# One decoder layer on one core: a new load order in the opening, sums moved to VectorE, a weight block loaded into its sum's tile, and a narrower widest level

## The chip, the cores and the metric

The kernel runs on one core of a Trainium2 chip. Five engines work side by side, each through its own queue in order: TensorE (PE in the profile, its weight loads PEld), VectorE (DVE), ScalarE (ACT), GpSimd (POOL) and SyncE (SP), which here only starts transfers. The metric is the device time of one execution in microseconds (us). The last section before the prediction gives the time before.

## The reference

One layer over 16 learned meta tokens and 1024 real ones, width 1024, in float32:

```
h = h + 1/2 * SwiGLU_1(RMSNorm(h))           # 1024 -> 2 x 2816 -> 1024
u = RMSNorm(h) @ W_in
o = concat[ HGRN2(u_hgrn), StickBreaking(u_sb) ]
h = h + o @ W_out
h = h + 1/2 * SwiGLU_2(RMSNorm(h))
```

HGRN2 has 4 heads of 128. Within a block of 128 positions it needs, for each query t and key s ≤ t, a score of q and k weighted by the product of the forget gates from s+1 to t:

```
decay = exp(bcum[t] - bcum[s])   where s <= t
attn  = einsum('td,sd,tsd->ts', q, k, decay)
o     = attn @ v + (q * exp(bcum)) @ S ;  S carried from block to block
```

Stick-breaking attention has 8 heads of 64. The output is the layer's h without the meta tokens.

## The kernel before, in words

Float32 products are made of three products of split operands: each operand x becomes a high part `xh` (an ACT cast) and a rest `xl` (a DVE subtraction), and PE adds wh·xh + wl·xh + wh·xl (`times`, L309; L599).

The 1040 positions are cut into a plain third of 272 and two wide ones of 384 (`THIRDS`). In both FFNs the two wide halves are multiplied by a Strassen-Winograd scheme: seven products of half-size blocks in place of eight. It needs sums of weight blocks (S1 = A21 + A22, S2 = S1 − A11, A11 − A21, A12 − S2) and sums of the operand's blocks (T1 to T4). In `fast_in` (the FFN's first product) a *quad* is seven such products, each 12 matmuls of 384 columns; a *pair* is a gate quad and an up quad. POOL makes the weight sums of `fast_in` (`made`, L281). When a pair is complete, `combined` (L435) makes four sums of its activations, T1 to T4, each followed by a store that POOL issues (`put`).

**The opening** (L1384 to L1437). The plain rows are loaded, normalised and turned (`first_plain`). The plain third is then multiplied for the first five pairs, block by block (`plain_quad`): 40 steps of 12 matmuls of 272 columns, each with a weight block of 256 KB from a ring of eight. In between, the rows of the two wide blocks are loaded (`rows_of`, three tiles of 128 rows each, on SP), normalised (`norm_rows`: a sum of squares for each tile, then for all three together one square root on ACT and a reciprocal, then one scaling on DVE for each tile) and turned by PE (`first_block`: 24 transposes for a block, in groups of 6, two plain steps between groups). Each block has its own root. Then the five *opened* pairs run over the wide blocks, and after them the other pairs with plain and wide parts together.

**What sets the order.** PE's instructions stand in the order in which they are written out. For the other engines and for SP's transfers a planner orders the instructions by its own costs, by priority (`high_priority`) and by when a tile comes free; `issue_after(x)` puts what is written inside it behind x on x's engine. So a load on SP's queue can stand in front of one that is needed sooner, and a load that waits for a tile holds up what is behind it.

**The FFN's second product** (`fast_out`, L491). Seven steps (A12, A11, S1, S2, S4, S3, A22), each eleven blocks long, each block with a weight tile and an activation tile. `raw` (L506) loads a weight block into a ring of five tiles (six in the second FFN). `left` (L525) gives a step its operand; A11 blocks are loaded straight into the wide tile `ak`, S1 is made into the wide tile `sk` from two ring tiles (L537), and S2 is made from both (L540).

**HGRN2** (`hgrn_attend`, L825) makes the scores of a block level by level: level n covers, in each stretch of 2n positions, the keys of the first half and the queries of the second. `scores` (L851) multiplies all 128 keys of a block by all 128 queries for four blocks into one score tile (pool `pz`, two tiles), and `level` (L870) copies out what belongs to the level, for n ≥ 16 by ACT (L877). After each level q and k are multiplied by the gates' products on DVE. Three heads run side by side, the fourth after the first, woven by `weave` with the first half of the mixing product (`mix_out`), whose operand `oT` is loaded from memory (L1649, three tiles).

**Before the second FFN** the rows are normalised by `row_norm` (L227), which multiplies by the row `g2r` of gains; that row is loaded by `gain_row` (L222) where it is first needed (L1709).

Of the kernel before, what the change touches and what calls it, by code (L numbers as in the profile page):

```python
# [20 lines left out]
P = 128  # L21
# [18 lines left out]
class Block:  # L40
# [212 lines left out]
    def fast_in(self, ops, n, w_in, actD, openers, ev0, open_ev, feed=None, plain=None,  # L253
# [19 lines left out]
        def block(i, h, col):  # L273
            t = self.wraw.tile([P, 4, P], F32, tag="raw", name="raw", bufs=self.in_bufs)
            self.last_w = nc.sync.dma_start(
                t, w_in[512 * h : 512 * h + 512, col + P * i : col + P * i + P]
                .rearrange("(k p) f -> p k f", p=P)
            )
            return t
# [122 lines left out]
        def pair(f, opened=None, also=(None, None)):  # L402
            sg = {}
# [31 lines left out]
            def combined():  # L435

                sub = nc.gpsimd.tensor_sub
# [53 lines left out]
    def fast_out(self, out_of, n, w_out, actD, load_h, ready, between=lambda a, q: None,  # L491
# [33 lines left out]
        def left(step, q):  # L525
# [10 lines left out]
            if step == "S1":  # L536
                nc.vector.tensor_add(s, raw(1, 0, q), raw(1, 1, q))  # L537
                return s
# [77 lines left out]
    def load_rows(self, eng, row, r0, m, cols=slice(0, D)):  # L616

        x, meta = self.a["x"][0], self.a["meta_tokens"]
        if r0 == 0:
            eng.dma_start(row[:META], meta[:, cols])  # L620
            eng.dma_start(row[META:m], x[: m - META, cols])
        else:
            eng.dma_start(row[:m], x[r0 - META : r0 - META + m, cols])

    def rows_of(self, ci, pool, eng):
# [3 lines left out]
        for r0 in range(c0, c0 + n, P):  # L629
            m = min(P, c0 + n - r0)  # L630
            row = pool.tile([P, D], F32, tag="row", name="row", bufs=self.row_bufs)
            self.load_rows(eng, row, r0, m)
# [23 lines left out]
    def norm_rows(self, ci, rows, junk, whole=False):  # L656

        nc = self.nc
        sums = self.ss[:, 3 * ci : 3 * ci + 3]

        def square(i, row, m):
            s = sums[:m, i, 0:1]
            if i == (1 if whole else 2):
# [13 lines left out]
        for i, (row, at, m) in enumerate(rows):  # L677
# [4 lines left out]
        if whole:  # L682
            root(P, slice(0, 3))
            for i, (row, at, m) in enumerate(rows):
# [140 lines left out]
    def hgrn_attend(self, h, pool, src, oH):  # L825
# [43 lines left out]

        def level(i, n):  # L870
            nb = P // (2 * n)
# [480 lines left out]
    def run(self):  # L1352
# [20 lines left out]
        with ExitStack() as c0:  # L1373
            with ExitStack() as c1:
                with tc.manual_schedule(engines={nc.tensor.engine}), ExitStack() as c2:
# [28 lines left out]

                    steps = self.fast_in(
# [7 lines left out]
                    with tc.high_priority():  # L1413
                        with tc.issue_after(self.last_w.ins):
                            rows.append(self.rows_of(2, rp, nc.sync))
                        with tc.issue_after(self.last_x.ins):
                            self.norm_rows(2, rows[1], junk, True)
                    drain(islice(steps, 4))
                    with tc.high_priority():
                        with tc.issue_after(self.last_w.ins):  # L1420
                            rows.append(self.rows_of(1, rp, nc.sync))
                        with tc.issue_after(self.root.ins):
                            self.norm_rows(1, rows[2], junk, True)
# [429 lines left out]
```

## Time and profile before

| | |
|---|---|
| runs | 2064.38, 2059.65, 2064.20 us; median 2064.2 |
| the profiled execution's own time | 2062.77 us |
| its span, first to last instruction | 2061.0 us |
| granted TensorE clock, mean | 1.000 |
| busy: PE, DVE, ACT, POOL | 2004.8, 1376.6, 901.2, 638.6 us |
| chain that ended last: PE, DVE, DMA | 83%, 7%, 3% |

The stages of this execution follow from the timeline: the plain steps of the opening from 14 to 86 us, the opened pairs from 86 to about 241, the other pairs to about 489; the first FFN's second product from 489 to about 710, its S1 step from about 600; projections and stick-breaking to about 1215; HGRN2 woven with the first half of the mixing product to about 1365; the second half with the norm to about 1420; the second FFN from there, its second product from 1847.

How to read a row: a line of the timeline gives start, length, engine, line of the kernel, operation, output and inputs, and in brackets the idle time just ahead of it with the engine and instruction that ended it. A row of grouped instructions gives how many there are, then busy time, mean length in ns and the idle time ahead of them. A row of waits gives who waited for whom: us in total, times, longest. PE's matmuls are pipelined, so the recorded length of one is longer than the distance to the next; distances between starts tell its pace.

### The profile page before, as it was taken

The page shows a single profiled execution, that of the slowest core. Times are in us where ns is not written, and L with a number is a line of the kernel's source. Part 1 is how long each engine was busy: PE and PEld are TensorE (multiplying, and loading weights), DVE is VectorE, ACT ScalarE, POOL GpSimd, SP SyncE. Part 2 cuts the span into 40 slices and gives each one's busy share as a digit, 9 for nine tenths or more (in the row PEclk, how much of TensorE's full clock was granted, in tenths as well). Part 3 has the DMA queues.
Part 4 walks back from the last instruction along what each step waited for, and adds up shares of the span by engine and source line. Part 5 has one row for each costly group of instructions (what it writes and reads, how often), then busy time and mean ns, then how long its engine had stood idle before and what let it go on. Part 6 is the DMA issues. An engine that isn't in the chain of part 4 may idle for free.

```text
span 2061.0 us, 31571 instructions
## 1 busy us (share of the span) xinstructions
PE 2004.8 (97%) x11249; PEld 1782.3 (86%) x11249; DVE 1376.6 (67%) x2069; ACT 901.2 (44%) x1855; POOL 638.6 (31%) x696
## 2 busy tenths in 40 slices
PE   7999999999999999999999999999999999999999
PEld 7999999999987899988887878888888888878887
DVE  6867745556688842257878757648677677666774
ACT  7633332334554534456666623336333333234443
POOL 2366644542000002243443300210564454441000
PEclk9999999999999999999999999999999999999999
DMA  8643322227875645435454262684343333349573
GB/s 237 192 145 113 112 79 94 99 76 232 285 219 171 226 135 169 147 123 130 116 144 114 64 223 88 195 272 137 112 131 105 95 110 102 97 150 346 185 229 113
DMA packets 289647, 314.96 MB, mean 153 GB/s; under 512 B 24080, under 2 KB 218000, under 8 KB 289488
## 3 DMA queue, kind: packets, MB, share of 16 engines
q1 hardware_dynamic: 272304, 260.83, 41.1%
q0 software_dynamic: 16144, 52.10, 6.6%
q8 instruction: 89, 1.46, 0.3%
q14 instruction: 70, 0.57, 0.1%
q10 hardware_dynamic: 1040, 0.00, 0.0%
HBM read 228.62 MB, written 84.23 MB: 152 GB/s over the span
## 4 chain that ended last, share of the span: by engine, by line
PE 83%; DVE 7%; DMA 3%; ACT 3%; issue 2%; POOL 0%; SPq 0%; DVEq 0%; POOLq 0%; ACTq 0%
PE o L599 16%; PE qb L313 15%; PE qa L313 10%; PE qc L313 10%; PE proj L162 5%; PE proj L160 5%; PE proj L161 5%; PE qd L313 4%; PE o L561 3%; PE wo L1267 3%; PE flip L1086 2%; DVE wl L270 1%; PE lvl L855 1%; DVE keep L1232 1%; PE oacc L1156 1%
## 5 line engine op out<-in xcount | busy, mean ns | idle before, releaser
L313 PE MATMUL qb<-T,wh 128*128 128x384 f32 (+1 forms) x1056 | 317.8, 362 | 0.0
L270 DVE TENSOR_TENSOR wl<-s,wh 128x512 fp32r<-128x512 f32 x176 | 198.8, 1130 | 95.2 <-ACT wh L268 91.1
L313 PEld LDWEIGHTS qb<-T,wh 128*128 128x128 f32 x1056 | 195.8, 188 | 21.5
L313 PE MATMUL qa<-B,wh 128*128 128x384 f32 (+1 forms) x704 | 213.9, 367 | 0.3 <-ACT sg L415 0.3
L599 PE MATMUL o<-wl,th 128*128 128x512 f32 x539 | 209.9, 391 | 3.7 <-DVE wl L520 3.7
L599 PE MATMUL o<-wh,tl 128*128 128x512 f32 x539 | 209.6, 390 | 0.7 <-DVE tl L520 0.7
L599 PE MATMUL o<-wh,th 128*128 128x512 f32 x539 | 209.9, 391 | 0.0
L268 ACT CAST wh<-s 128x512 fp32r<-128x512 f32 x176 | 109.4, 621 | 223.2 <-PE qb L313 164.1
L160 PE MATMUL proj<-xh,wh 128*128 128x384 f32 (+2 forms) x576 | 205.0, 356 | 0.2 <-ACT xh L250 0.2
L270 DVE TENSOR_TENSOR wl<-raw,wh 128x512 fp32r<-128x512 f32 x184 | 170.1, 926 | 52.2 <-ACT wh L268 48.7
L161 PE MATMUL proj<-xh,wl 128*128 128x384 f32 (+2 forms) x576 | 199.1, 346 | 0.0
L162 PE MATMUL proj<-xl,wh 128*128 128x384 f32 (+2 forms) x576 | 198.9, 345 | 0.1
L268 ACT CAST wh<-raw 128x512 fp32r<-128x512 f32 x184 | 113.6, 620 | 184.1 <-PE qc L313 100.4
L313 PE MATMUL qb<-T,wl 128*128 128x384 f32 (+1 forms) x528 | 192.0, 364 | 0.9 <-DVE wl L270 0.9
L518 ACT CAST th<-act 128x512 fp32r<-128x512 f32 (+2 forms) x176 | 96.6, 550 | 178.1 <-PE o L599 120.0
L520 DVE TENSOR_TENSOR tl<-act,th 128x512 fp32r<-128x512 f32 (+2 forms) x176 | 105.5, 602 | 64.9 <-ACT th L518 63.7
L313 PE MATMUL qd<-X,wh 128*128 128x272 f32 x704 | 144.4, 292 | 2.0 <-DVE sp L397 1.6
L283 POOL TENSOR_TENSOR s<-raw 128x512 f32<-128x512 f32 x88 | 122.6, 1393 | 74.8 <-DVE wl L270 60.1
L313 PEld LDWEIGHTS qa<-B,wh 128*128 128x128 f32 x704 | 130.5, 188 | 16.5 <-ACT sg L415 0.7
L1232 DVE TENSOR_TENSOR_SCAN keep<-keep 128x144 f32<-128x144 f32 (+6 forms) x112 | 127.1, 1138 | 8.3 <-ACT keep L1228 6.0
L1237 POOL TENSOR_TENSOR sig<-sig,keep 128x144 f32<-128x144 f32 (+3 forms) x64 | 88.2, 1378 | 141.7 <-DVE keep L1232 75.6
L313 PE MATMUL qa<-B,wl 128*128 128x384 f32 (+1 forms) x352 | 128.8, 366 | 0.8 <-DVE wl L270 0.8
(343 smaller groups left out, 4761.1 us busy)
## 6 DMA issues: line engine op xcount, KB each, us to landing
raw<-in_ffn_w_in_dram SPq DMA_DIRECT2D x228, 256.0 KB, 3.0
raw<-in_ffn_w_out_dram SPq DMA_DIRECT2D x176, 256.0 KB, 4.3
raw<-in_w_in_dram SPq DMA_DIRECT2D x28, 512.0 KB, 4.5
ks<-kD SPq DMA_DIRECT2D x32, 260.0 KB, 5.6
oT<-oD SPq DMA_DIRECT2D x32, 256.0 KB, 4.7
ak<-in_ffn_w_out_dram SPq DMA_DIRECT2D x22, 256.0 KB, 5.3
v<-vD SPq DMA_DIRECT2D x8, 576.0 KB, 4.8
vD<-vhl SPq DMA_DIRECT2D x8, 512.0 KB, 3.9
```

The source lines that it names most:

```text
L160: nc.tensor.matmul(ps, wh[:, s], xs, start=k == 0, stop=False)
L161: nc.tensor.matmul(ps, wl[:, s], xs, start=False, stop=False)
L162: nc.tensor.matmul(ps, wh[:, s], xl[:, k, c0 : c0 + n], start=False, stop=k == nk - 1)
L268: nc.scalar.copy(hi, src)
L270: nc.vector.tensor_sub(lo, src, hi.bitcast(F32))
L283: op(t, x, y)
L313: nc.tensor.matmul(ps, a[:, k, :], b[:, k0 + k, :], start=start and k == 0 and i == 0, stop=k == 3 and i == 2, skip_group_check=True,)
L518: nc.scalar.copy(hi, src)
L520: nc.vector.tensor_sub(lo, src, hi.bitcast(F32))
L599: nc.tensor.matmul(banks[bank][m], z[:, m * P : (m + 1) * P], y, start=start and q == 0 and e == 0, stop=q == nq - 1 and e == 2, skip_grou ...
L1232: nc.vector.tensor_tensor_scan(out=kv, data0=kv, data1=kv, initial=1.0 if last else keep[:, end : end + 1], op0=ALU.mult, op1=ALU.bypass,)
L1237: nc.gpsimd.tensor_mul(sig, sig, keep[:, 1 : nk + 1])
```

## The change

- *Opening.* Both wide blocks' rows are loaded before either is normalised: the second block's (`ci` 2) after the first eight steps' weights, the other's after the next four steps'. Weight loads written after a block's rows stand behind these on SP's queue (`rows_ahead`, the last row's load). `norm_rows` takes all six row tiles: two of the six sums of squares are on DVE, four on ACT, and there is one root over six columns.
- *Opened pairs.* Their four sums are made by DVE in place of POOL; the stores stay on POOL's queue. The later pairs and the second FFN keep POOL.
- *S1.* The block A21 is loaded straight into its place in `sk`, and A22 from the ring is added to it there; in both FFNs.
- *Widest level* (n = 64). 64 keys by 64 queries for each of the eight blocks, into one score tile of 64 partitions, and one copy in place of two.
- *Before the second FFN.* The row `g2r` is loaded ahead of HGRN2, into the pool that holds h; `oT` has four tiles instead of three.

```diff
         def block(i, h, col):
             t = self.wraw.tile([P, 4, P], F32, tag="raw", name="raw", bufs=self.in_bufs)
-            self.last_w = nc.sync.dma_start(
-                t, w_in[...].rearrange("(k p) f -> p k f", p=P)
-            )
+            with ExitStack() as behind:
+                if self.rows_ahead:
+                    behind.enter_context(self.tc.issue_after(self.rows_ahead.ins))
+                self.last_w = nc.sync.dma_start(
+                    t, w_in[...].rearrange("(k p) f -> p k f", p=P)
+                )
             return t
...
         def pair(f, opened=None, also=(None, None)):
+            opening = plain and also == (None, None)
...
-                sub = nc.gpsimd.tensor_sub
+                sub = (nc.vector if opening else nc.gpsimd).tensor_sub
...
             if step == "S1":
-                nc.vector.tensor_add(s, raw(1, 0, q), raw(1, 1, q))
+                nc.sync.dma_start(s, block(1, 0, q))
+                nc.vector.tensor_add(s, s, raw(1, 1, q))
                 return s
...
-    def norm_rows(self, ci, rows, junk, whole=False):
+    def norm_rows(self, at, rows, junk, whole=False):
-        sums = self.ss[:, 3 * ci : 3 * ci + 3]
+        sums = self.ss[:, at : at + len(rows)]
-            if i == (1 if whole else 2):
+            if i % 3 == (1 if whole else 2):
-            root(P, slice(0, 3))
+            root(P, slice(0, len(rows)))
...
+        def widest():
+            ps = self.pz.tile([P // 2, 8, P // 2], F32, tag="z", name="lvl")
+            for c in range(8):
+                s = META + c * P
+                nc.tensor.matmul(
+                    ps[:, c, :], KB[:, s : s + P // 2], QA[:, c * P + P // 2 : (c + 1) * P],
+                    start=True, stop=True,
+                )
+            nc.scalar.copy(at8[: P // 2, :, P // 2 :], ps)
+
         def level(i, n):
+            if 2 * n == P:
+                return widest()
...
-                    with tc.high_priority():
-                        with tc.issue_after(self.last_w.ins):
-                            rows.append(self.rows_of(2, rp, nc.sync))
-                        with tc.issue_after(self.last_x.ins):
-                            self.norm_rows(2, rows[1], junk, True)
-                    drain(islice(steps, 4))
-                    with tc.high_priority():
-                        with tc.issue_after(self.last_w.ins):
-                            rows.append(self.rows_of(1, rp, nc.sync))
-                        with tc.issue_after(self.root.ins):
-                            self.norm_rows(1, rows[2], junk, True)
+                    for ci in (2, 1):
+                        with tc.high_priority(), tc.issue_after(self.last_w.ins):
+                            rows.append(self.rows_of(ci, rp, nc.sync))
+                        self.rows_ahead = self.last_row
+                        if ci == 2:
+                            drain(islice(steps, 4))
+                    with tc.high_priority(), tc.issue_after(self.last_x.ins):
+                        self.norm_rows(3, rows[1] + rows[2], junk, True)
...
                     hb = self.pool("hb", ctx=c1)
+                    gain = self.gain_row(a["ffn2_norm"][0:1], hb, "g2r")
...
-                        t = self.pool_o.tile([P, 2, 4, P], F32R, tag="oT", name="oT", bufs=3)
+                        t = self.pool_o.tile([P, 2, 4, P], F32R, tag="oT", name="oT", bufs=4)
...
-                    gain = self.gain_row(a["ffn2_norm"][0:1], pn, "g2r")
```

More of the change, by code (lines that the diff above doesn't have):

```diff
@@ L274, in block @@
             t = self.wraw.tile([P, 4, P], F32, tag="raw", name="raw", bufs=self.in_bufs)
-            self.last_w = nc.sync.dma_start(
-                t, w_in[512 * h : 512 * h + 512, col + P * i : col + P * i + P]
-                .rearrange("(k p) f -> p k f", p=P)
-            )
+            with ExitStack() as behind:
+                if self.rows_ahead:
+                    behind.enter_context(self.tc.issue_after(self.rows_ahead.ins))
+                self.last_w = nc.sync.dma_start(
+                    t, w_in[512 * h : 512 * h + 512, col + P * i : col + P * i + P]
+                    .rearrange("(k p) f -> p k f", p=P)
+                )
             return t
@@ L620, in load_rows @@
             eng.dma_start(row[:META], meta[:, cols])
-            eng.dma_start(row[META:m], x[: m - META, cols])
-        else:
-            eng.dma_start(row[:m], x[r0 - META : r0 - META + m, cols])
+            return eng.dma_start(row[META:m], x[: m - META, cols])
+        return eng.dma_start(row[:m], x[r0 - META : r0 - META + m, cols])
     def rows_of(self, ci, pool, eng):
@@ L631, in rows_of @@
             row = pool.tile([P, D], F32, tag="row", name="row", bufs=self.row_bufs)
-            self.load_rows(eng, row, r0, m)
+            self.last_row = self.load_rows(eng, row, r0, m)
             got.append((row, r0 - c0, m))
@@ L675, in root @@
             nc.vector.reciprocal(r, r)
-        for i, (row, at, m) in enumerate(rows):
+        for i, (row, _, m) in enumerate(rows):
             square(i, row, m)
@@ L682, in norm_rows @@
         if whole:
-            root(P, slice(0, 3))
-            for i, (row, at, m) in enumerate(rows):
+            root(P, slice(0, len(rows)))
+            for i, (row, _, m) in enumerate(rows):
                 nc.vector.tensor_scalar_mul(row, row, sums[:, i, 1:2])
@@ L1403, in between @@
                         next(turning[0], None)
+                    self.rows_ahead = None
                     steps = self.fast_in(
@@ L1431, in run @@
                             next(steps)
+                    self.rows_ahead = None
                     drain(steps)
```

## The prediction

> **What bounds the kernel now.** I read the page first, then the tensor engine's waits by stage, then the timeline of the engine that each wait names.
>
> ```profile
> span 2061.0 us, 31571 instructions
> PE 2004.8 (97%) x11249; PEld 1782.3 (86%) x11249; DVE 1376.6 (67%) x2069; ACT 901.2 (44%) x1855; POOL 638.6 (31%) x696
> ```
>
> The tensor engine (PE) is busy 97% of the span, so there are two ways to gain: close one of its holes, of which there are 2061.0 − 2004.8 = 56 us in all, or give it less to do. The change touches five places with holes. The profiled execution took 2062.77 us, 1.8 around its span, and the median of the runs is 2064.2; the sum is made against 2062.77, and a change is judged against 2064.2. About 0.3%, 6.2 us, is what a measurement of this kernel can tell from none.
>
> **A. The opening's load order and the single root.** Its two larger holes are 0.94 + 1.63 = 2.6 us:
>
> ```profile
> 31.66 0.39 PE L313 MATMUL qd<-X,wl 128*128 128x272 f32 x1 [0.94 <-DVE wl L270]
> 49.28 0.36 PE L313 MATMUL qd<-X,wh 128*128 128x272 f32 x1 [1.63 <-DVE sp L397]
> 20.00:40.00 20.00, 19.06 (x152) 18.84 (x152) 13.41 (x33) 14.63 (x27) 5.49 (x11) 1.00 0.89 276
> 40.00:60.00 20.00, 17.94 (x139) 16.91 (x138) 17.59 (x38) 19.27 (x39) 1.63 (x3) 1.00 0.59 150
> 25.11 1.06 ACT L668 ACTIVATE junk<-row 128x1024 bf16<-128x1024 f32 x1
> 26.79 1.28 ACT L672 ACT_TABLE_LOAD   x1
> 28.09 0.30 ACT L672 ACTIVATE ss_x<-ss_x,eps 128x3 f32<-128x3 f32 x1
> 33.48 0.46 SPq L623 DMA_DIRECT2D row<-in_x_dram  x1
> row<-in_x_dram SPq DMA_DIRECT2D x7, 512.0 KB, 5.3
> 34.66 0.82 PE L648 MATMUL xps<-ident,row 128*128 128x128 f32 x6
> ```
>
> (The window rows give start:end, length, then busy time and count of PE, PEld, DVE, ACT and POOL, the granted clock, the DMA share and GB/s.) The larger hole falls in 40 to 60 us, where ACT is busy 19.27 of 20.00 us and DVE 17.59. The second block's squares, root and scaling are done there; the change moves them forward, and two roots become one. That removes a root (0.30) and two table loads of 1.28 (to the root's table and back), 2.9 us of ACT's work where it is full. [...]
>
> The price is on the first block: its scaling now waits until the sixth row tile has landed. On SP's queue the new order is eight weight blocks, three row tiles, four weight blocks, three row tiles, the rest. Up to the sixth tile that is 1.1 MB (the plain rows) + 12 × 0.26 + 6 × 0.52 = 7.4 MB, at 276 GB/s 26.8 us of transfer: it lands at 28, or somewhat later. A square (1.06) and the table load (1.28) then put the root at about 31 instead of 28.09. In the trace 6.6 us pass from the root's start to the transposes at 34.66; with as much again they would come at 38 at the latest, where the tensor engine arrives at 33.7 if the first hole is gone. So the new hole is 0 to 4.3 us; I take 1.4, since the transposes take the tiles one after another, and 2.0 of the old holes recovered: **0.6**. The ends are 0.94 − 4.3 = −3.4 and 2.6. Weight blocks queued behind rows are covered by the eight that are loaded ahead.
>
> **B. The opened pairs' sums on VectorE.**
>
> ```profile
> PE qc L313 <- DVE wl L270: 1.9, 1, 1.9
> PE qb L313 <- DVE wl L270: 0.9, 3, 0.4
> PE qc L313 <- DVE sg L417: 0.5, 3, 0.2
> 123.20 1.31 POOL L283 TENSOR_TENSOR s<-raw,s 128x512 f32<-128x512 f32 x1
> 124.46 1.01 POOL L444 TENSOR_TENSOR t<-sg,t 128x384 f32<-128x384 f32 x1
> 125.44 1.28 POOL L283 TENSOR_TENSOR s<-raw 128x512 f32<-128x512 f32 x1
> 123.79 3.48 DVE L270 TENSOR_TENSOR wl<-raw,wh 128x512 fp32r<-128x512 f32 x1 [1.07 <-ACT wh L268]
> 132.80 0.69 DVE L270 TENSOR_TENSOR wl<-raw,wh 128x512 fp32r<-128x512 f32 x1
> 126.72 0.34 PE L313 MATMUL qb<-T,wh 128*128 128x384 f32 x1
> 127.33 0.44 PE L313 MATMUL qb<-T,wl 128*128 128x384 f32 x1 [0.27 <-DVE wl L270]
> L427 DVE TENSOR_TENSOR sg<-u,sg 128x384 f32<-128x384 f32 x14 | 7.7, 551 | 0.0
> L440 POOL DMA_DIRECT2D act10T<-t x3: 547/552/552, 119.6 to 126.7; - x3
> DMA to landing us min/median/max: 2.1/2.1/2.2
> ```
>
> From 85 to 241 us the tensor engine waits seven times in the gate half of a pair, while POOL catches up with the previous pair's four sums. At 123.79 a subtraction that takes 0.69 us alone takes 3.48: it ends as the third of POOL's three adjoining instructions does. The recorded idle is 3.3 us; start to start a stall costs more (126.72 to 127.33 is 0.61, where 0.17 is usual, so 0.44 against 0.27), seven times 0.17 more: 4.4. The change takes 4 × 1.01 us a pair off POOL and adds 4 × 0.55 = 2.2 us a pair to DVE, for which a pair's 14 steps of 12 × 0.17 = 2.1 us have room. POOL's weight sums stay and still slow DVE, so I take **3.0** of 4.4. [...]
>
> The fourth sum needs the first one's tile back (two buffers): its store is issued by POOL (0.55) and lands 2.1 us later, so DVE may stand up to 0.55 + 2.1 − 1.1 (the two sums between) = 1.6 us there, with weight subtractions and evictions behind it. Three buffers of weights, two steps of 2.1 us ahead, cover that. Lower end 0; the uncovered case is a rival.
>
> **C. The block loaded into its sum's tile.**
>
> ```profile
> 600.00:610.00 10.00, 9.37 (x44) 7.39 (x43) 7.31 (x13) 5.22 (x11) 1.08 (x2) 1.00 0.94 312
> 620.00:630.00 10.00, 9.35 (x40) 6.95 (x39) 10.00 (x18) 4.95 (x10) 0.00 (x0) 1.00 0.59 187
> 630.00:640.00 10.00, 9.10 (x40) 6.99 (x39) 10.00 (x19) 4.25 (x9) 0.00 (x0) 1.00 0.30 86
> 580.00:590.00 10.00, 10.00 (x46) 8.29 (x45) 10.00 (x23) 7.41 (x16) 0.00 (x0) 1.00 0.24 64
> DVE sk L537 <- DMA raw<-in_ffn_w_out_dram: 7.3, 3, 3.9
> 1848.31 205.91 PE o L599 x907
> ```
>
> In the first FFN's S1 step DVE waits 7.3 us for blocks: each sum takes two of the ring's five tiles, so only two and a half steps are ahead. Afterwards DVE is full (10.00) while it catches up. At 580 to 590 the tensor engine runs 46 matmuls in 10 us; the three later stretches are short of that by 2 + 6 + 6 = 14, at 205.91/907 = 0.227 us each 3.2. With the first block in the sum's own tile the ring holds five steps. I take **2.6**, the waits and most of the catching up; ends 0 and 3.2. The eleven blocks, 2.9 MB, now load earlier; at 580 to 590 the DMA engines are at 0.24, and that is the cover. Without it they would take 2.9 MB / 312 GB/s = 9 us of transfers, in front of loads that the ring has five steps of 9 × 0.227 = 2.04 us ahead. In the second FFN the chain is 907 matmuls without a break: nothing to gain there.
>
> **D. The widest level by 64 keys.**
>
> ```profile
> 1248.67 12.81 PE L855 MATMUL lvl<-QA,KB 128*128 128x128 f32 x104 [0.18 <-DVE attn L886]
> L1156 PEld LDWEIGHTS oacc<-wu,v 128*128 128x128 f32 x160 | 30.7, 192 | 0.9
> L1158 PEld LDWEIGHTS oacc<-wu,v 128*64 128x64 f32 x160 | 21.8, 136 | 0.8 <-DVE wu L1201 0.2
> 1261.84 4.73 PE L855 MATMUL lvl<-QA,KB 128*128 128x128 f32 x40 [0.36 <-ACT attn L877]
> 1339.79 1.16 PE L855 MATMUL lvl<-QA,KB 128*128 128x128 f32 x8 [0.94 <-ACT attn L877]
> L877 ACT COPY attn<-lvl 64x256 f32<-64x256 f32 x8 | 2.9, 367 | 3.8 <-PE lvl L855 3.7
> ```
>
> A level is 8 matmuls, 16 records, at 12.81/104 = 0.123 us each. No row has an f32 matmul of 64 by 64. Weight loads of 64 columns against 128 take 136 against 192 ns, 56 less, and half the queries should take about as much off the streaming: 4 heads × 16 × 0.056 = 3.6 us. The ends are 0 (a record costs what it did, or a chain on DVE and ACT hides it) and 3.6 + 0.36 + 0.94 = 4.9, since one score tile instead of two needs no second one freed by ACT's copies. Two copies of 367 ns become one of at most 0.73. I take **3.2**: one head's share may hide behind DVE.
>
> **E. The gain row earlier and a fourth oT tile.**
>
> ```profile
> 1365.38 0.50 PE L1267 MATMUL wo<-wh,oT 128*128 128x512 f32 x1 [1.02 <-DMA oT<-oD]
> 1383.09 0.50 PE L1267 MATMUL wo<-wh,oH 128*128 128x512 f32 x1 [0.63 <-DVE hm L1693]
> 1210.00:1220.00 10.00, 9.60 (x68) 8.05 (x66) 5.94 (x15) 2.80 (x5) 0.00 (x0) 1.00 1.02 400
> ```
>
> The first hole is a load that waited for a tile; the second is an eviction behind a normalisation that waited for the gain row. Together 1.65, with refill up to 2.0. The gain row's 0.5 MB moves in front of the mixing stage, past SP's loads there, into a stretch already at 400 GB/s: 1.3 us of transfer, −1.3 if it delays the heads' loads. I take **1.2**.
>
> **The sum.** 0.6 + 3.0 + 2.6 + 3.2 + 1.2 = 10.6; 2062.8 − 10.6 = **2052.2**, 12 below the median. All upper ends together give 17.1 (2045.7), all lower ends −4.7 (2067.5).
>
> **The rivals.** *The sixth tile lands late.* If it lands as today's last one does, issued at 33.48 and 5.3 us on its way, the root comes at about 41 and the transposes, 3 us after it, at 44 instead of 34.66. A is then −9.5 instead of 0.6, and the time 2062 to 2063. For it: today SP spreads these loads up to 33.48. Against it: that order was the planner's, and the new one is written out. Chance 0.10.
> *DVE takes over as the limit.* Where DVE is full (10.00 from 620 to 640) earlier loads only move its backlog, and in B it gets more work: C gives 0.5, B 1.0, and 0.6 + 1.0 + 0.5 + 3.2 + 1.2 = 6.5, so 2056.3. Against it: DVE stood idle 7.3 us just before. It stands also for blocks that the planner loads no earlier than now. Chance 0.22.
> *Slower: DVE and POOL wait for each other in the pairs.* POOL's stores T1 to T4 now wait for DVE, DVE's fourth sum waits for POOL's first store, and POOL's weight sums for the next gate half are queued behind those stores. With two weight sums of 1.3 us in front of the store the 1.6 us become 4.2, and POOL's later weight sums are late by as much again; of these 8.4 the cover takes 4.2. At 3 us a pair five pairs lose 15, and with the other terms' 7.6 the time is 2070. Slower than before by 0.3% it is from (7.6 + 6.2)/5 = 2.8 us a pair. Chance 0.06.
>
> **How the numbers follow.** My forecast has 0.62, its own range 2047 to 2057. The range reaches 2046 to 2062, to take in the second rival and most of the first. Faster by over 0.3% means below 2058: nearly all of the forecast (0.58) and over half of the second rival (0.14), 0.72. The rest of these two (0.04 and 0.08) and most of the first rival (0.09) make 0.21 for no change; the third and the end of the first, 0.07, are slower.
>
> **What would show it.** A: one root of six columns, near 32 us, no hole of 1.6 us at 49, a hole of at most 2.5 before the first wide transposes. B: no 3.48 us subtraction, and the seven waits gone from 85 to 241 us. C: no wait of DVE for the S1 blocks, 46 matmuls per 10 us through S1 and S2. D: records of the widest level about 0.06 us apart. E: neither wait. The forecast is wrong if new waits on DVE appear in the pairs, if the root ends after 35 us, or if the widest level's records stay at 0.12.

## The result and the profile after

| | before | after |
|---|---|---|
| median of the runs | 2062.9 us (6 runs, 2059.7 to 2066.3) | 2051.3 us (6 runs, 2049.2 to 2056.6) |
| the profiled execution, its span | 2062.8, 2061.0 us | 2051.4, 2049.2 us |
| ratio | | 0.9947, 95% interval 0.9931 to 0.9963 |

The change makes the kernel 11.5 us faster; 2052.2 was predicted. But the terms of the sum were not as predicted. From TensorE's timeline, start to start of the same matmuls:

| stage (matmul it begins with) | before | after | gained | predicted |
|---|---|---|---|---|
| plain steps of the opening (first plain matmul) | 71.63 | 69.29 | 2.3 | A 0.6 |
| opened pairs (first wide matmul) | 156.63 | 151.02 | 5.6 | B 3.0 |
| other pairs, first steps of the second product | 351.99 | 352.19 | -0.2 | 0 |
| S1 to the end of that product (first transpose of the plain result) | 130.89 | 126.55 | 4.3 | C 2.6 |
| projections, stick-breaking (first projection matmul) | 490.54 | 492.05 | -1.5 | 0 |
| HGRN2, mixing, norm (first score matmul) to the second FFN | 203.75 | 203.16 | 0.6 | D and E 4.4 |
| second FFN, to the last matmul | 636.93 | 636.97 | 0.0 | 0 |

Three terms came out larger than forecast, and the last stage, for which 4.4 us were expected, gave 0.6. The sum is 11.1; the two spans differ by 11.8, and most of the rest lies behind the last matmul.

The page of the changed kernel:

```profile
span 2049.2 us, 31558 instructions
PE 2001.5 (98%) x11249; PEld 1782.7 (87%) x11249; DVE 1368.1 (67%) x2088; ACT 898.4 (44%) x1848; POOL 619.9 (30%) x676
```

TensorE's holes are 47.7 us in all instead of 56.2, and its busy time is 3.3 less.

The opening, from the timelines of TensorE, ScalarE and SP:

```profile
29.93 0.39 PE L316 MATMUL qd<-X,wl 128*128 128x272 f32 x1 [0.75 <-DVE wl L270]
34.45 0.38 PE L652 MATMUL xps<-ident,row 128*128 128x128 f32 x2
35.20 0.44 PE L652 MATMUL xps<-ident,row 128*128 128x128 f32 x2 [0.37 <-DVE row L689]
35.86 0.44 PE L652 MATMUL xps<-ident,row 128*128 128x128 f32 x2 [0.23 <-DVE row L689]
...
29.78 1.28 ACT L676 ACT_TABLE_LOAD   x1
31.07 0.30 ACT L676 ACTIVATE ss_x<-ss_x,eps 128x6 f32<-128x6 f32 x1
...
18.80 1.41 SPq L627 DMA_DIRECT2D row<-in_x_dram  x3
```

There is one root of six columns, at 31.07. The second group of row loads is issued by 20.2, so that the sixth tile is no late one. The first wide transposes start at 34.45 (34.66 before), and the hole between them, priced at 1.4, is 0.37 + 0.23. The hole of 1.63 at 49 has no successor; the first one, 0.94 before, is still 0.75 (29.93).

The opened pairs and S1, from the timelines of VectorE and POOL and from the windows:

```profile
210.63 1.49 POOL L286 TENSOR_TENSOR s<-s,raw 128x512 f32<-128x512 f32 x1
210.89 1.78 DVE L270 TENSOR_TENSOR wl<-raw,wh 128x512 fp32r<-128x512 f32 x1
212.06 0.55 POOL L444 DMA_DIRECT2D act13T<-t  x1
...
600.00:610.00 10.00, 10.00 (x45) 8.28 (x45) 10.00 (x19) 5.18 (x10) 0.00 (x0) 1.00 0.36 101
610.00:620.00 10.00, 10.00 (x45) 8.26 (x44) 10.00 (x19) 5.18 (x10) 0.00 (x0) 1.00 0.41 118
620.00:630.00 10.00, 10.00 (x46) 8.28 (x45) 6.69 (x12) 5.10 (x10) 0.00 (x0) 1.00 0.32 99
```

1.78 us is the longest a weight subtraction takes in the opened pairs (4.14 before), and TensorE has no recorded wait there. In S1 VectorE is as full as before, 10.00, but TensorE no longer waits for it.

HGRN2, where the gain went, from TensorE's timeline, before (three rows) and after, and after in windows of 3.41 us:

```profile
1270.75 1.95 PE L855 MATMUL lvl<-QA,KB 128*128 128x128 f32 x16
1275.88 0.48 PE L934 MATMUL s<-vm,kms 16*128 16x128 f32 x2 [0.67 <-DVE F L944]
1276.74 1.83 PE L941 MATMUL up<-vr,vT 128*128 128x128 f32 x14 [0.38 <-DVE F L935]
...
1258.62 1.15 PE L878 MATMUL lvl<-QA,KB 128*64 128x64 f32 x16
1259.69 0.48 PE L950 MATMUL s<-vm,kms 16*128 16x128 f32 x2
1260.11 2.18 PE L957 MATMUL up<-vr,vT 128*128 128x128 f32 x14
1263.36 0.48 PE L950 MATMUL s<-vm,kms 16*128 16x128 f32 x2 [1.07 <-DVE F L960]
1265.11 2.44 PE L957 MATMUL up<-vr,vT 128*128 128x128 f32 x14 [1.27 <-DVE F L951]
1270.81 0.63 PE L1283 MATMUL wo<-wl,oT 128*128 128x512 f32 x1
1271.24 1.05 PE L1283 MATMUL wo<-wh,oT 128*128 128x512 f32 x2
1273.20 0.39 PE L1283 MATMUL wo<-wl,oT 128*128 128x512 f32 x1
1273.43 0.39 PE L1283 MATMUL wo<-wh,oT 128*128 128x512 f32 x1
1273.66 0.38 PE L970 MATMUL op<-F,QA 128*128 128x128 f32 x2
...
1262.74:1266.15 3.41, 1.52 (x11) 1.33 (x12) 2.28 (x7) 0.62 (x1) 0.00 (x0) 1.00 0.36 108
1266.15:1269.56 3.41, 2.73 (x14) 2.14 (x13) 2.62 (x8) 0.00 (x0) 0.00 (x0) 0.50 0.15 52
1269.56:1272.97 3.41, 3.41 (x12) 2.83 (x11) 0.00 (x0) 1.17 (x2) 0.00 (x0) 0.50 0.35 121
```

Up to the first state matmul (`up`, 1260.11) the stage takes 55.17 us in place of 57.47: 2.3 won. From there to the first output matmul (`op`) it takes 13.55 in place of 10.33: 3.2 lost. Two things lie in between: the waits for F on VectorE (a head's states, block by block) have grown from 0.67 + 0.38 to 1.07 + 1.27, and then the granted clock is 0.50 for 6.8 us, so that a 512-wide matmul comes 0.43 us after the one before (1270.81 to 1271.24) where 0.23 is usual (1273.20 to 1273.43). From there to the second FFN the stage wins 1.5. Both waits that E named (1.02 and 0.63) are gone there, and one of 0.65 for VectorE's `res` has come.

### The profile page after: what moved, and what is told of

The parts are those of the page before. It is cut to its first block, busy times and chain, and to the rows that moved or that the text cites. A ratio compares the mean times of both kernels' runs of the same rounds, so it can differ in the third digit from the quotient of the medians.

```text
span 2049.2 us, 31558 instructions
## 1 busy us (share of the span) xinstructions
PE 2001.5 (98%) x11249; PEld 1782.7 (87%) x11249; DVE 1368.1 (67%) x2088; ACT 898.4 (44%) x1848; POOL 619.9 (30%) x676
## 4 chain that ended last, share of the span: by engine, by line
PE 86%; DVE 6%; issue 3%; ACT 3%; DMA 2%; POOL 1%; SPq 0%; DVEq 0%; POOLq 0%; ACTq 0%
PE o L604 17%; PE qb L316 16%; PE qa L316 10%; PE qc L316 10%; PE proj L160 5%; PE proj L162 5%; PE proj L161 5%; PE qd L316 4%; PE o L566 3%; PE wo L1283 3%; PE flip L1102 2%; PE lvl L859 1%; DVE keep L1248 1%; PE oacc L1172 1%; PE oacc L1174 1%
## 5 line engine op out<-in xcount | busy, mean ns | idle before, releaser
L270 DVE TENSOR_TENSOR wl<-s,wh 128x512 fp32r<-128x512 f32 x176 | 188.1, 1069 | 89.4 <-ACT wh L268 85.1
L270 DVE TENSOR_TENSOR wl<-raw,wh 128x512 fp32r<-128x512 f32 x184 | 158.3, 862 | 49.0 <-ACT wh L268 45.2
```

Of the source, the lines that this page charges most:

```text
L270: nc.vector.tensor_sub(lo, src, hi.bitcast(F32))
```

## The experiments

The stages above are the measure, each from one execution of a kernel. Where kernels have the same code, the opened pairs and the second FFN repeat within 0.1 us; the opening varies by 0.9, the first and the last steps of the first FFN's second product by 1.1 and 1.8, projections with stick-breaking by 1.7, and HGRN2's stage by 1.5 (202.75 to 204.21 in the four kernels that have it as changed).

### The opened pairs' sums on POOL again

```diff
-                sub = (nc.vector if opening else nc.gpsimd).tensor_sub
+                sub = nc.gpsimd.tensor_sub
```

> The changed kernel with the opened pairs' four sums back on GpSimd; all else as changed. Theory (the sums on GpSimd stand back to back with its weight sums, and a VectorE subtraction that runs into such a row waits until the row ends): subtractions of about 3.5 us return at three of the pairs, and the stretch from the first wide step (83.1) to the end of the opened pairs (234.2) grows from 151.0 us by the whole 5.6 that it lost, to about 156.6; the time is 2051.3 + 5.6 = 2057. Rival one (part of the 5.6 came from the new opening, whose loads reach the first pair earlier): it grows by the 4.9 of the pairs alone or less, and the wait of 0.5 at the first wide step stays away. Rival two (VectorE's own order, not GpSimd's load, made the stalls): no subtraction over 1.8 us, and under 1 us of growth. The two waits on GpSimd's sums in the first FFN's other pairs are not touched by either.

Measured: the opened pairs take 156.31 us, 5.3 more, between the theory's 5.6 and the first rival's 4.9; 2059.2 us (2054.4 to 2062.2, 10 runs). VectorE's timeline and TensorE's waits from 80 to 240 us of this kernel:

```profile
121.42 3.48 DVE L270 TENSOR_TENSOR wl<-raw,wh 128x512 fp32r<-128x512 f32 x1 [1.07 <-ACT wh L268]
152.44 3.48 DVE L270 TENSOR_TENSOR wl<-raw,wh 128x512 fp32r<-128x512 f32 x1 [1.07 <-ACT wh L268]
215.01 3.61 DVE L270 TENSOR_TENSOR wl<-raw,wh 128x512 fp32r<-128x512 f32 x1 [0.94 <-ACT wh L268]
...
PE qc L316 <- DVE wl L270: 1.9, 1, 1.9
PE qb L316 <- DVE wl L270: 0.9, 3, 0.4
PE qc L316 <- DVE sg L421: 0.5, 3, 0.2
```

The long subtractions (these three, and one of 4.15 at 182.59) and all seven waits are back, while the wait of 0.51 at the first wide matmul stays away, as the first rival had it: that 0.3 belongs to the new opening. The recorded idle is 3.3, the loss 5.3: the stalls here cost 1.6 times what their rows show. In the kernel before, the subtraction at 123.79 ends at 127.27, 0.55 after the third of POOL's three adjoining instructions (126.72) and 0.03 after the start of POOL's next weight sum (127.24). In the changed kernel, where POOL's weight sums stand apart, the longest, from 210.89, ends 0.55 after the one sum that it overlaps (210.63 to 212.12) and takes 1.78. What holds the long ones up is not shown.

### S1 from two ring tiles again, and a larger ring

```diff
-                nc.sync.dma_start(s, block(1, 0, q))
-                nc.vector.tensor_add(s, s, raw(1, 1, q))
+                nc.vector.tensor_add(s, raw(1, 0, q), raw(1, 1, q))
```

> The changed kernel with S1 = A21 + A22 made again from two ring tiles, in both FFNs. Theory (the ring held two and a half S1 steps, so VectorE stood still and then ran behind): VectorE's waits for the blocks return (7.3 us before, three times), TensorE's waits on the split parts come back in three places of the steps S1 and S2, and from the first S1 step to the end of the first FFN's second product 4.2 to 4.3 us are lost; second FFN unchanged within 0.3; the time about 2051.3 + 4.3 = 2055.6. Rival (the waits came from where the transfers happened to stand in the kernel before, and the new opening and pairs moved them): under 2 us lost, with VectorE's wait under 4 us.

Measured: 131.05 us in place of 126.55, 4.5 lost; second FFN 636.99; 2054.0 us (7 runs). The waits, VectorE's from 585 to 640 us and TensorE's from 585 to 655, are those of the kernel before:

```profile
DVE sk L541 <- DMA raw<-in_ffn_w_out_dram: 7.4, 4, 3.7
...
PE o L603 <- DVE wl L524: 2.2, 3, 1.1
```

The other half of the question, ring or transfers, was put to the kernel before:

```diff
-            t = ring.tile([P, 512], F32, tag="raw", name="raw", bufs=self.ring_bufs)
+            t = ring.tile([P, 512], F32, tag="raw", name="raw", bufs=6)
```

> The kernel before with six ring tiles for weight blocks in the first FFN's second product in place of five; S1 from two ring tiles as before. Theory (how many steps the ring holds decides: three in place of two and a half, where the changed kernel has five): VectorE's wait for S1's blocks falls from 7.3 to 4 us or less, and from the first 512-wide S1 step on 1 to 3 of the 4.3 us are won (131 us fall to 128 to 130). Rival (the blocks' transfers or VectorE's own backlog decide, not the ring): under 0.5 us is won and the waits for the blocks stay above 6 us.

Measured: VectorE's wait for the blocks falls from 7.3 to 3.0 us, and the stretch that had the stalls (the 181st to the 360th of the product's matmuls of 512 columns) takes 41.7 us, against 45.7 before and 41.4 in the changed kernel and the nine others with its S1. So the depth of the ring is what counted, by 4.0 us. The kernel itself is slower, 2074.2 us: the second product starts late, and why is not shown. TensorE's wait there, after which the granted clock is 0.50 for 10.24 us:

```profile
PE o L561 <- ACT th L518: 7.7, 1, 7.7
```

In the last steps another 3.5 us are lost, so that the whole stretch shows only 0.5 won (130.43). The change's way, a tile that is there anyway, had no such price.

### The widest level by 128 keys again, and alone

```diff
-            if 2 * n == P:
-                return widest()
```

> The changed kernel with the widest level again by 128 keys and 128 queries in two score tiles. The records themselves are 0.9 us shorter a head (1.15 instead of 2.05 for sixteen). Theory (the gain is real in the first three heads, 3.1 us up to the first state matmul, and most of it is then given back to VectorE, whose chain F has to end first): the stretch from the first flip to the first state matmul (56.1 us) grows by 2.3 to 3.0, but from the first flip to the first matmul of the second FFN the loss is only 0.5 to 1.5; the time 2051.8 to 2052.8. Rival (what was given back was a short fall of the granted clock, 0.81 and 0.85 in two windows of 10 us there, and not VectorE): with the clock at 1.00 there, the loss up to the second FFN against a run without such a fall is 3 us or more.

Measured: to the first state matmul 57.47 (2.3 more), from there to the first output matmul 10.33 (3.2 less), and from the first score matmul to the second FFN 201.48 us, against 203.16 in the changed kernel and 203.75 before. Taking the narrow level away wins 1.7 us of the stage (1.3 to 2.7 against the four executions that have it). The expectation had a loss of 0.5 to 1.5; its rival, that the clock takes the gain, has more right. The kernel's time is 2051.8 (4 runs), not to be told from the changed kernel's 2051.3. Then the level alone was put into the kernel before:

```diff
         def level(i, n):
+            if 2 * n == P:
+                return widest()
```

> The kernel before with the narrower widest level alone. Theory (the shorter level brings TensorE to the state matmuls 2.3 us earlier; there VectorE still has subtractions of mixing weights in front of the chain F, TensorE's waits for F grow from 2.0 to about 2.7 us, a stretch of 3.4 us then has TensorE busy less than 1.7 us, and the granted clock is halved for one or two stretches of 3.4 us): the first flip to the first state matmul takes 56.1 instead of 58.4 us, from there to the first output matmul 12.2 to 13.6 us instead of 10.3, the clock is 0.5 for 3.4 or 6.8 us from about 1277, and the time is 0 to 1.5 us above the kernel before's. Rival (the fall of the clock goes with the gain row or the fourth oT tile, not with the level): 10.3 to 11.0 us there, the clock at 1.00, and 2 us won.

Measured: 55.15 to the first state matmul, 13.48 from there, the clock at 0.83 in both windows of 10 us from 1270 on and 0.66 from 1340 on; the stage takes 208.74 us, 5.0 more than before. But this execution, 2068.2 us, is the slowest of the ten; their median is 2064.1 against 2064.7, between which the runs can't tell, so neither a gain nor a loss of the level alone is shown. The fall does go with the level, and not with the gain row or the oT tile: between the first state matmul and the first output matmul it is in the traces of all six kernels here whose level is narrow and whose order on VectorE is as it was (mean granted clock 0.996 to 0.998), and of none of the five whose sixteen records take 1.95 us or more. TensorE's timeline and its waits from 1200 to 1425 us:

```profile
1274.35 0.48 PE L946 MATMUL s<-vm,kms 16*128 16x128 f32 x2 [1.07 <-DVE F L956]
1276.02 2.82 PE L953 MATMUL up<-vr,vT 128*128 128x128 f32 x14 [1.18 <-DVE F L947]
...
PE lvl L874 <- DVE KB L920: 3.9, 1, 3.9
PE wo L1279 <- DVE hm L1705: 1.2, 1, 1.2
```

Eight falls stand in the traces of the changed kernel and of the runs with POOL sums, two ring tiles, the full widest level and the late gain row, in HGRN2 or in stick-breaking. In the changed kernel the changes of the clock at 1081.83, 1085.24, 1266.15 and 1272.97 lie 1, 53 and 2 times 3.41 us apart. Counted in steps of that length, TensorE was busy for 1.1 to 1.6 of 3.41 us just ahead of each of the eight (1.56 and 1.52 in the changed kernel), and the clock was 0.50 after it. No step ahead of the eight was idle: the longest single wait ahead of the fall at 1266.15 is 1.27 us. A step nearly as low does not always bring a fall: one with 1.65 at 1057.94 in the changed kernel passes at 1.00, as do those with 1.74 at 187.44 and 1.79 at 1139.76 in the kernel before. In both kernels TensorE is busy for only 1.14 of some 3.41 us in stick-breaking (from 1138.0 before, from 1127.4 after), but the two steps that share this stretch have 2.76 and 1.79 before, 2.26 and 2.29 after, and no fall follows. At 1078.42 after, one step has 1.56, and 0.50 follows for 3.41 us; by estimate (half of 3.41) that takes 1.7, and projections with stick-breaking took 1.5 longer. At HGRN2's end no 3.41 us have less than 2.10 in the kernel before.

### The gain row late again

```diff
-                    gain = self.gain_row(a["ffn2_norm"][0:1], hb, "g2r")
...
+                    gain = self.gain_row(a["ffn2_norm"][0:1], pn, "g2r")
```

> The changed kernel with the gain row loaded where it was before, by the second half of the mixing product, and four oT tiles kept. Theory (the row's 0.5 MB in front of the heads' loads puts off the mixing weights, whose casts and subtractions then fall into the heads' chain on VectorE): ScalarE's cast of a mixing weight no longer waits 2.2 us at the end of the heads, the waits for F shrink from 1.07 + 1.27 to under 1.2 in all, and the wait of 0.6 before the last eviction of the mixing product returns; 0.5 to 1.5 us won there, 1.0 lost later; the time within 1 us of 2051.3. Rival (the row costs nothing where it stands now): the waits for F stay as they are, and 0.6 to 1.0 us are lost at the norm.

Measured: the waits for F stay at 1.07 and 1.29, ScalarE's cast still waits 2.30 us for a mixing weight, and the clock falls all the same; at the norm 1.62 us are back, and the stage takes 204.58, 1.4 more, which is 0.4 above the slowest of the four executions with the early row. The row costs nothing where it stands, the rival's case; how much more than the wait of 1.62 it is worth is not shown. The time is 2054.6 (10 runs), 3 us above the changed kernel where within 1 was expected, though the intervals of the two ratios still overlap (0.9950 to 0.9975 and 0.9931 to 0.9963). No run takes the fourth oT tile back alone, so its share is not shown. TensorE's timeline at the norm:

```profile
1373.86 0.50 PE L1283 MATMUL wo<-wh,oH 128*128 128x512 f32 x1 [1.62 <-DVE hm L1708]
```

### Two roots with the new load order

```diff
-                        self.norm_rows(3, rows[1] + rows[2], junk, True)
+                        self.norm_rows(3, rows[1], junk, True)
+                        self.norm_rows(6, rows[2], junk, True)
```

> The changed kernel with the new load order of the opening but a root of its own for each wide block. Theory (the opening won its 2.3 us because both blocks' rows come early and their squares, roots and scalings leave the stretch from 40 to 60 us, where ScalarE was full; that two roots became one is a small part): the hole of 1.6 us at 49 stays away, and from the first plain step to the first wide step it takes 69.3 to 70.2 us (71.6 before, 69.3 with one root). Rival (the one root, with its 0.30 and two table loads of 1.28, was what counted, 2.9 us of ScalarE): more than 1.0 us comes back, over 70.3 us, and it shows as a TensorE wait between 30 and 50 us.

Measured: 70.35 us, just beyond the line drawn between the two; the hole at 49 stays away, and a new one of 0.92 at 30.23 waits for ScalarE, which has loaded a table in front of it; another of 1.34 stands at 26.05. Without the change this stage took 70.98 to 71.63 (three kernels), with it 69.29 to 70.19 (ten). So the term is 1.6 on average, of which the load order and the single root may have about half each; with a spread of 0.9 the split is not shown.

### What stands in front of the chain

On VectorE the wait for F has this order in the changed kernel:

```profile
1261.21 0.68 DVE L147 TENSOR_TENSOR wl<-raw,wh 128x512 fp32r<-128x512 f32 x1
1261.81 1.94 DVE L960 SCALAR_TENSOR_TENSOR F<-F,Ts,up 128x128 f32<-128x128 f32 x5
1263.90 0.69 DVE L147 TENSOR_TENSOR wl<-raw,wh 128x512 fp32r<-128x512 f32 x1 [0.15 <-ACT wh L145]
1264.52 0.34 DVE L960 SCALAR_TENSOR_TENSOR F<-F,Ts,up 128x128 f32<-128x128 f32 x1
1264.77 0.28 DVE L951 COPY F<-s 128x128 f32<-128x128 f32 x1
```

Two subtractions of mixing weights, which nobody needs yet, stand in front of the sums F and of the copy for which TensorE waits. With three raw tiles for these weights the second goes:

```diff
-                    self.weights("wo", 2, 8, c1)
+                    self.weights("wo", 3, 8, c1)
```

> The changed kernel with three tiles instead of two for the raw mixing weights, so that they are loaded and split earlier: on VectorE the second of the two subtractions no longer stands between the chain's F operations. Theory (that subtraction makes the wait of 1.3 us for the copy F, and this wait brings TensorE below half busy and so the clock down): the wait for the copy falls under 0.5 us, the clock stays at 1.00 from 1260 to 1280, first state matmul to first output matmul 10.3 to 11.3 us instead of 13.6, and 2.0 to 3.0 us are won against the changed kernel: 2048.3 to 2049.3. Rival (the clock falls whatever waits for what there, since the level is shorter): it falls again to 0.5 and under 1 us is won.

Measured: the copy is waited for 0.4 us, the clock stays at 1.00 there, and from the first state matmul to the first output matmul it takes 10.93 us. But the fourth head's widest level now waits 2.7 for KB, behind another late subtraction, and the stage takes 201.99: 1.2 won, not 2 to 3; 2050.4 us (5 runs), which the runs can't tell from the changed kernel. Then the chain itself was put first:

```diff
+            with self.tc.high_priority() if n >= 16 else nullcontext():
                 nc.vector.tensor_mul(
                     qa[:, :, 1, :], qa[:, :, 1, :],
...
+        with self.tc.high_priority():
             nc.vector.tensor_copy(S[:, 0, :], ps)
...
+                with self.tc.high_priority():
                     nc.vector.scalar_tensor_tensor(
                         S[:, c + 1, :], S[:, c, :], dec[:, 1 + c : 2 + c], ps[:, j, :],
```

> As the run with three raw tiles, and on VectorE the chain of the heads (the products of QA and KB from level 16 on, the copies F and the sums F) is put ahead of what else is ready, so that no subtraction of a mixing weight stands between the chain's operations in the first three heads. Theory (each subtraction in front of the chain costs its 0.7 us and whatever it waits for itself): TensorE's wait for F before the second head's state falls from 1.3 to 0.7 us or less, first state matmul to first output matmul 10.0 to 10.5 us (10.9 with three raw tiles, 13.6 in the changed kernel), no fall of the clock from 1260 to 1280; in the fourth head one late subtraction still stands in front of KB, so its wait of about 2.7 us stays. From the first score matmul to the second FFN 201.0 to 201.5 us, against 203.2 in the changed kernel. Rival (TensorE waits for its own earlier matmuls and the two tiles of the pool, whatever VectorE's order): 10.9 us or more.

Measured: 10.25 us to the first output matmul, with a wait of 0.92 for F before the second state where 0.7 or less was expected, and the stage takes 198.76, better than forecast, since the wait for KB went too. TensorE's timeline and the window:

```profile
1263.32 0.48 PE L951 MATMUL s<-vm,kms 16*128 16x128 f32 x2 [0.92 <-DVE F L963]
1264.19 1.83 PE L959 MATMUL up<-vr,vT 128*128 128x128 f32 x14 [0.38 <-DVE F L953]
...
1260.00:1270.00 10.00, 7.40 (x51) 6.01 (x50) 6.66 (x19) 1.75 (x3) 0.00 (x0) 1.00 0.39 122
```

2047.0 us (2046.3 to 2047.5, 4 runs), ratio to the kernel before 0.9913 (0.9898 to 0.9928): 4.3 us below the changed kernel, whose interval (0.9931 to 0.9963) it does not touch, and the best of the kernels here. Both levels were compared in it:

> The kernel of the run with the heads' chain first, with the widest level again by 128 keys and 128 queries. Theory (with the chain clear of other work the narrow level is worth its 2.3 us in the first three heads, and no fall of the clock takes them back): from the first score matmul to the first output matmul the wide level takes 2.0 to 2.6 us longer than that kernel (65.5 us against 68 in the kernel before). From there on the fourth head's wait for KB is under 1 us, since the longer level gives the late subtraction time, so that up to the second FFN both differ by under 1 us. Rival (the chain on VectorE sets the pace whatever the level's length): the difference up to the first output matmul is under 1 us.

Measured: 67.99 instead of 65.40 us to the first output matmul, 2.6 more, and 201.40 instead of 198.76 for the stage; 2050.0 us (2049.5 to 2051.0, 4 runs), clear of the 2047.5 of the slowest run with the narrow level. With the chain clear, the narrow level is worth 2.6 us, and nothing gives it back. (That the two meet again at the second FFN was expected and is wrong.)

### Which side has to be narrow

At every level only the scores of the later half of the queries are used:

```diff
+            ps = self.pz.tile([P, 8, nb, n], F32, tag="z", name="lvl")
+            for c in range(8):
+                nc.tensor.matmul(
+                    ps[:, c], KB[:, META + c * P : META + (c + 1) * P],
+                    later(QA[:, c * P : (c + 1) * P], n), start=True, stop=True,
+                )
```

> The kernel with the heads' chain first, and at every level the 128 keys are multiplied by the 64 later queries of a block alone, into one score tile, with one masked copy in place of two. TensorE's scores fall by 0.9 us a level and head. Theory one (VectorE is busy 9.9 of 10 us from 1210 to 1240, so it sets the pace there, and it gains only the few hundredths of a microsecond that one long copy saves over two): the first score matmul to the first state matmul gets shorter by 0.5 to 2 us only, with TensorE busy about 6 of 10 us in place of 9. Theory two (where TensorE is busy less than half of a stretch of 3.4 us the clock is halved): the narrow levels bring such stretches, the clock falls to 0.5 in one or more of them between 1210 and 1250, and nothing or less than nothing is won. Rival (TensorE set the pace in the levels): 4 us or more are won.

Measured: 78.37 us to the first state matmul, 23 more than with the chain first; 2075.7 us (7 runs), slower than before (1.0047, 1.0027 to 1.0066). What theory two forecast came, but not in the way it said: sixteen records still take up to 2.00 us at the full clock, so TensorE is no less busy, and the clock falls nevertheless. Its limit of half a stretch was the author's estimate from the earlier falls (1.1 to 1.6 of 3.41 us), and no run shows it. The windows show the last stretches before the fall at 1229.8 and what follows:

```profile
1225.41 2.00 PE L891 MATMUL lvl<-QA,KB 128*128 128x64 f32 x16 [0.16 <-DVE attn L903]
...
1222.71:1226.12 3.41, 3.25 (x29) 3.11 (x29) 3.41 (x6) 0.00 (x0) 0.00 (x0) 1.00 0.63 153
1226.12:1229.53 3.41, 2.74 (x25) 2.60 (x25) 3.41 (x6) 0.00 (x0) 0.00 (x0) 1.00 0.00 0
1229.70:1233.11 3.41, 3.21 (x17) 3.03 (x16) 3.41 (x7) 0.00 (x0) 0.00 (x0) 0.51 0.02 5
```

The clock stays at 0.50 until 1274, for 44 us; by estimate (half of 44) the fall takes 22 us, about what was lost. The last run asks which side sets a record's length:

```diff
+                    nc.tensor.matmul(
+                        ps[:, j, :], KB[:, s : s + P // 2], QA[:, c * P : (c + 1) * P],
```

> The kernel with the heads' chain first, and at the widest level 64 keys by all 128 queries of a block, into two score tiles: the weights are narrow (64 columns), the streamed side is not. So far, sixteen records take 2.05 us by 128 keys and 128 queries, 1.15 by 64 and 64, and 2.00 by 128 keys and 64 queries (in the run with the later queries at every level). Theory (the number of weight columns sets the pace, and the number of queries only shows where the weights are narrow too): sixteen records in 1.2 to 1.4 us. Rival (each side alone can hold the pace: a record takes as long as the longer of the weight load and the streaming): 1.9 to 2.05 us, so that the level is worth anything only with both sides narrowed. Either way up to the second FFN within 2 us of the kernel with the chain first, 2047 to 2050 us.

Measured: sixteen records take 1.96 us, the rival's case, and the stage 201.05 us, as with the wide level (201.40); 2049.7 us (4 runs). TensorE's timeline:

```profile
1260.77 1.96 PE L880 MATMUL lvl<-QA,KB 128*64 128x128 f32 x16
```

The wide level's own sixteen take 1.95 to 2.05, so that 1.96 and 2.00 are no shorter; only 64 by 64 gives 1.15.

## Why the prediction was right, and where it was not

The time was right because errors of both signs cancelled.

- **A, mis-sized.** The mechanism held: the hole at 49 went and the transposes did not move. Predicted were 0.6, measured 2.3 in this trace and 1.6 over the kernels. The step that failed is the price of the first block's scaling, 1.4 for the hole at the transposes, which was 0.6. It took "as much again" of 6.6 us from the root to the transposes; from 31.07 to 34.45 it is 3.4. The row at 34.66 could have said so: it has no idle time ahead of it, so TensorE came to it from its own plain steps and waited for no scaling. Of the first hole, 0.94, only 0.2 went.
- **B, mis-sized.** All seven waits went, and none came for VectorE, as the step said. No run shows the lower end of the term, 0: the opened pairs gained 5.6, and lost 5.3 with their sums on POOL again. But 3.0 was a discount on 4.4 for weight sums that "still slow DVE", and 4.4 itself (its terms, 3.3 and seven times 0.17, give 4.5) was too low an upper end: the stalls were worth 5.3.
- **C, mis-sized.** The ring was the reason, as the run with six tiles shows. The term was 3.2 and was cut to 2.6, on three stretches of the table; counted from start to start over S1 and S2 (the 181st to the 360th matmul) it is 4.2.
- **D, wrong.** The records got as short as forecast (1.15 for sixteen). The step that failed is that only "one head's share may hide behind DVE": the chain F on VectorE ends last there, the waits for it left TensorE busy for 1.52 of 3.41 us, and the granted clock was 0.50 for the 6.8 us after that; by estimate (3.2 lost, less 1.3 by which the waits grew) the lower clock took 1.9. In place of +3.2 the level cost 1.7 in this kernel's stage, and alone it changed the time by nothing that the runs show (5.0 lost in the slowest of ten). Only with the chain put first is it worth 2.6.
- **E, mis-sized.** 1.2 was predicted; 2.3 is the stage's difference between the kernel before and the one with the wide level and all else changed (203.75 and 201.48). The two waits vary by themselves: 1.02 and 0.63 in the kernel before, 0.5 and 1.8 in the same code of the run with six ring tiles. The lower end, loads delayed by the row, did not occur.
- **Not in the sum at all:** the 1.5 us that projections and stick-breaking lost, with the granted clock at 0.50 for 3.41 us from 1081.83. Six of the kernels with the change have such a fall at about 1080, the rest elsewhere or not at all. Whether it is a price of the change or chance is open: nine of the eleven traces with the change have one in stick-breaking, and so has one of the three without it, the kernel before with six ring tiles (at 1081.96). In 54 further executions of the kernel before the mean granted clock is 1.000 only twice and 0.997 to 0.999 otherwise; the trace that the sum was made against has no fall at all.
- **The rivals.** The sixth tile was not late. VectorE does not take over in S1: it is full from 570 to 620, and TensorE does not wait. The wait of both for each other in the pairs did not appear. The second rival's words fit one place, for which it was not written: D.

## What to carry to other kernels

When a stage gets shorter, look at what is queued on the other engines in front of the chain that now ends last: an operation that nobody needs yet, such as a weight's subtraction, can stand there unseen until then, and moving it (4.4 us of HGRN2's stage) was worth more than the shorter level itself (2.6). The stalls cost more than their idle rows here (5.3 for 3.3), so a table of starts of the same matmuls before and after is the better scale. And waits of 1.07 and 1.27 us cost more than their length here: they left TensorE busy for 1.52 of 3.41 us, and the granted clock was 0.50 for the next 6.8 us, by estimate 1.9 us more.

## What was not expected of the hardware

- In the changed kernel the granted clock was 0.50 for 3.41 us from 1081.83 and for 6.8 us from 1266.15, after steps of 3.41 us in which TensorE was busy for 1.56 and 1.52, with no wait longer than 1.3 us at 1266. Steps with 1.65 at 1057.94 there, and with 1.74 at 187.44 in the kernel before, passed at 1.00. After TensorE's wait of 7.7 us in the run with six ring tiles the clock was 0.50 for 10.24 us.
- Recorded busy time alone does not tell when it fell: in the run with the later queries at every level (128 weight columns, 64 streamed ones) it fell after stretches of 3.25 and 2.74 of 3.41 us, and stayed at 0.50 for 44 us. What it goes by is open: a plain count of the streamed columns does not order the steps either (2336 ahead of the fall at 1081.83 in the changed kernel, 1664 with no fall from 1256.20 in the last run).
- Sixteen float32 records of a level were shorter only with both sides narrow: they take 1.95 to 2.05 us at 128 by 128, 1.89 to 2.00 at 128 keys by 64 queries, 1.96 at 64 by 128, and 1.15 at 64 by 64.
